# Modulation units dealt anew under the in-projection of layer 0, with the statistics, states and reload of layer 1 in new places

## The chip, the cores and the metric

The kernel runs on one core of a Trainium2 chip. The metric is the device time of one execution in microseconds (us). Engines are called as in the profile: PE is the matrix engine (TensorE), PEld its weight loads, DVE the vector engine, ACT the scalar engine, POOL is GpSimd, and SP issues most DMAs. Each engine works through its own queue in order; semaphores tie the queues together.

## The reference, cut to what matters

Two layers work on 512 latent rows and 256 context rows, both 2048 wide. Every layer is modulated: from the conditioning vectors come shift, scale and gate, `silu(c) @ ada_w[i] + ada_b[i]`, once for the latent rows and once for the context rows.

```python
for i in range(DEPTH):
    shift, scale, gate = jnp.split((sc @ ada_w[i] + ada_b[i])[:, None, :], 3, axis=-1)
    shift_c, scale_c, gate_c = jnp.split(scc @ ada_w[i] + ada_b[i], 3, axis=-1)
    h = rmsnorm(x, norm_w[i]) * (1.0 + scale) + shift
    hc = rmsnorm(xc, norm_w[i]) * (1.0 + scale_c) + shift_c
    ...
    x = x + gate * y
    if need_ctx:
        xc = xc + gate_c * yc
return rmsnorm(x, final_norm)
```

Layer 0 (`even_mix`) projects `h` and `hc` into a pool branch, its gate, low-rank queries and keys, and a gate of 1536 columns, then runs dense attention with 12 heads, and projects out. Layer 1 (`odd_mix`) projects into a bidirectional mLSTM with 4 heads (queries, keys, values, gates; the context rows give its initial states) and a window attention with 16 heads over 128-row windows plus the context keys, each with a Silu gate; then it projects out, for the latent rows alone.

## The kernel before, in words

Everything is computed transposed: features on the 128 partitions, rows along the free axis, in 16 chunks of 128 features. A float32 product is made of three matmuls with operands split into a high and a low half (`split`, lines 107 to 109: ACT writes the high half, DVE or POOL subtracts for the low half). Weights come in 512 KB pieces through `load_w` (line 111): three raw buffers, and four buffers each for high and low halves of half a piece.

**Modulation.** The columns of `ada_w` are cut into 24 units of 512 columns, 12 per layer. Units 0 to 7 (shift and scale of layer 0) are done on PE at the start. The others are done in one of two ways. `ada_pe_steps` (line 154) loads a unit in 16 pieces of 256 KB and multiplies them on PE, four pieces side by side in the array. `ada_vec_steps` (line 174) does it on DVE: per piece one `scalar_tensor_tensor` per conditioning vector adds the scaled piece to an accumulator (line 187), then a transpose and a reduction per accumulator (lines 192 and 193), and one tiny matmul folds the result (line 199). Units 20 to 23 (the gate of layer 1) need one vector alone, since layer 1 makes no context output: 17 steps with one operation each, where other units have 18 steps with two. A `Background` object (line 204) holds a row of such units; `bg.step(n)` at a place in the program text emits n steps there, `bg.finish()` the rest.

**In-projection of layer 0** (lines 480 to 603). `in_group(g, between, steps)` (line 505) does a group of 256 columns: four weight pieces, and for each 48 matmuls on 512 latent and 256 context rows, with `steps[0]` background steps before them and `steps[1]` behind. Order of groups: 2 and 3 (low-rank queries), 4 to 7 (pool branch and its gate, two and two, with the pool averages on DVE between), 8 to 13 (the attention gate). Before, the background of this stage held units 8 to 13, and groups 8 and 9 held units 18 and 19 on PE.

**Layer 0 to layer 1.** The out-projection of layer 0 adds into the residual and sums squares chunk by chunk on POOL, the last chunk on DVE (line 891). `stats1(v)` (line 926) turns the sums into one factor per row: tiny matmuls into `ps6b`, a root, and a broadcast by matmul. v is 0 for latent rows, 1 for context rows. `h_chunk` (line 278) then makes the modulated, normed, split input: HX for latent rows, HC for context rows. After that `x_group_t` (line 966) makes the mLSTM queries in two groups, from HX alone.

**mLSTM states.** `od_mv0`, the keys, then `mv_group` for value heads 1 to 3 and a last group with the window keys and values (lines 1199 to 1246). Between their weight pieces `next(state)` advances `ctx_state` (line 1214): scale the context values by their weights on DVE, split, six matmuls into `pc0`, split the result into `C0`; twice per head, for the two directions. Units 20 to 23 were the background of this stage.

**Window attention** (lines 1442 to 1701). A software pipeline over 4 head groups and 4 windows: scores of the next window (`Softmax.heads`), transposed probabilities and values of the present one (`w_values`), and between them `run(n)` takes n matmuls from `fillers()`: the query and gate projections of head groups 1 to 3 (`w_proj`), then the first out-projection groups (`out_steps`), which read Z, the split output of both branches. `z_load` (line 1558) reloads from DRAM the chunks of Z that are already made. `wq_split` (line 1458) rotates a finished query block (`do_rope`: shuffle, two products, a sum) and splits it.

The order of the instructions on each engine is settled when the program is built. A planner takes, by its own estimates of durations, the ready instruction that stands first in the program text; parts under `high_priority` go ahead, and where `manual_schedule` is set for PE (the window attention, the dense attention and the start), PE's order is the written one. Buffers of one tag are given out in turn. The planner does not see the chip: an instruction that is late there holds all that stands behind it in its queue.

Of the kernel before, what the change touches and what calls it, by code (L numbers as in the profile page):

```python
# [11 lines left out]
ALU = mybir.AluOpType  # L12
# [26 lines left out]
def tile_hybrid_dit(ctx: ExitStack, tc: tile.TileContext, ts: dict, out: bass.AP, dbg=None, upto=99):  # L39
# [94 lines left out]
    def ada_steps(u, pp, tp, nb=3, nt=2):  # L134

        pa = pp.tile([P, 512], F32, name=f"pa{u}", tag="pm")
        for q in range(4):
# [7 lines left out]
            if q == 3:  # L145
                tr = tp.tile([P, 16, 32], F32, name=f"ga{u}", tag="ga", bufs=1)
                V.transpose(tr.rearrange("p b r -> p (b r)"), pa)
                yield
                pb = pp.tile([32, 2, 16], F32, name=f"pb{u}", tag="pm")
                T.matmul(pb, fold, tr[:, :, 0:2].rearrange("p b v -> p v b"), start=True, stop=True)  # L150
                ada_place(u, pb, 2)
            yield

    def ada_pe_steps(u, pp, tp, nb):

        pa = pp.tile([P, 512], F32, name=f"pa{u}", tag="pm")
        for q in range(4):
            at = []
            for i in range(4):
                kc = 4 * q + i  # L160
                at.append(tp.tile([P, 512], F32, name=f"at{u}_{kc}", tag="ada", bufs=nb))
                DM.dma_start(at[i], ts["ada"][u, kc // 2][:, (kc % 2) * 512 : (kc % 2) * 512 + 512])
            for qd in range(4):
                T.matmul(pa[32 * qd : 32 * qd + 32, :], st[:, 4 * q + qd, :], at[qd], start=q == 0, stop=q == 3, skip_group_check=True)
            if q == 3:
                tr = ta("gat", 512).rearrange("p (b r) -> p b r", r=32)
# [162 lines left out]
    def do_rope(ps, r, tmp):  # L329
# [7 lines left out]
        G.tensor_tensor(t2, sw, rope[1], op=ALU.mult)  # L337
# [165 lines left out]
    bg = Background(range(8, 14), pp, ap_, 4, "ta", 6)  # L503
# [15 lines left out]
    for g in range(2):  # L519
        px, pc = in_group(2 + g, steps=(2, 2))  # L520
        raw += c_evac([(px[b], pc[:, b, :]) for b in range(2)], ssq)
# [50 lines left out]
    for pr in range(2):  # L572
        px, pc = in_group(4 + 2 * pr, steps=(1, 0))
# [9 lines left out]
        qx, qc = in_group(5 + 2 * pr, (lambda: mean(1), lambda: mix(0), lambda: None, lambda: mix(1)), (0, 0))  # L583
# [8 lines left out]
    for i in range(6):  # L592
        if i < 2:
            pe = ada_pe_steps(18 + i, pp, ap_, 4)
            px, pc = in_group(8 + i, (lambda: next(pe), lambda: next(pe), lambda: next(pe), lambda: (next(pe), next(pe))), (0, 0))
        else:
            px, pc = in_group(8 + i, steps=(2, 2))
# [344 lines left out]
    HX = [(hxp.tile([P, NX], F32R, name=f"hxh{j}"), hxp.tile([P, NX], F32R, name=f"hxl{j}")) for j in range(KC)]  # L942
# [33 lines left out]
    stats1(1)  # L976
    for j in range(KC):
        h_chunk(j, x1[j], ssq1, 12, 1, *((None, HC[j][i]) for i in range(2)), Ring(htp, 2), (1,))
    for i in range(2):
        for b, px in enumerate(x_group_t(G_MQ + i)):  # L980
# [214 lines left out]
    ea = ExitStack()  # L1195
    bg = Background(range(20, 24), pp, opool(ea, "ada1"), 4, "atr", 1)


    def mv_group(h, state):
        px, pc = new_px(2), new_pc()  # L1200
        pv = [px[b // 2][:, 256 * (b % 2) : 256 * (b % 2) + 256] for b in range(4)]
        for kq in range(4):
            w = load_w(odw[1 + h, kq])
            kcs = range(4 * kq, 4 * kq + 4)
            bg.step(2)
            kmode(pv, w, kcs, HX, kq == 0, kq == 3, 2)
            bg.step(3)
            kmode([pc[:, b, :] for b in range(2)], w, kcs, HC, kq == 0, kq == 3, 2)
            if kq % 2 == 0:
                next(state, None)  # L1210
# [28 lines left out]
    for kq in range(4):  # L1239
        w = load_w(odw[5, kq])  # L1240
        bg.step(2)
        tmode(px, [pc[:, b, :] for b in range(2)], w, range(4 * kq, 4 * kq + 4), HX, HC, kq == 0, kq == 3)
        if kq % 2 == 0:
            next(state, None)
    bg.finish()
    ea.close()
# [211 lines left out]
    def wq_split(src):  # L1458
        rr = ap2.tile([P, NX], F32, name="wrr", tag="wrr", bufs=1)
        do_rope(src, rr, rtmp(ap2))  # L1460
# [20 lines left out]
    def w_proj(i):  # L1481

        for g in (G_AQ + i, G_AZ + i):
# [5 lines left out]
            for kq in range(4):  # L1489
                w = load_w(odw[g, kq])  # L1490
                kcs = range(4 * kq, 4 * kq + 4)
                for b in range(2):
                    yield from steps(px, w, kcs, (b,), HX, kq == 0, kq == 3)
                    if kq == 3 and g < G_AZ:
                        qs[i] += wq_split(px[b])
                    elif kq == 3:
                        S.activation(zg[i][:, b, :], px[b], AF.Silu)
# [5 lines left out]
    class Softmax:  # L1503
# [7 lines left out]
        def heads(self, pair):  # L1511
# [12 lines left out]
            for a, s in zip(pair, ss_):  # L1524
                pr = wt("wpr_", 640)
                mx = tiny.tile([P, 1], F32, name="wm1", tag="wm1", bufs=4)
# [377 lines left out]
```

## Time and profile before

| | |
|---|---|
| three runs | 2303.32, 2305.13, 2306.37 us; median 2305.13 us |
| profiled execution | 2305.76 us, its span (first to last instruction) 2304.0 us |
| PE, PEld, DVE, ACT, POOL busy in the span | 2229.1, 1894.9, 1406.7, 916.3, 162.8 us |
| granted PE clock, mean | 0.993 |
| DMA | 309.14 MB, mean 134 GB/s |

A group's row reads: line, engine, operation, output <- inputs, shape, count, then busy time, mean duration in ns, and idle time of the engine before it. A wait's row reads: who waited <- for whom: us in total, times, longest. A timeline row reads: start, duration, engine, line, operation, count, and in brackets the idle time of the engine before it and what ended it. Matmuls are pipelined: one of 512 columns lasts 0.40 us in the records, but the next starts 0.23 us later.

### The profile page before, as it was taken

What the parts mean: (1) busy time and instruction counts of PE and PEld (TensorE: products, weight loads), DVE (VectorE), ACT (ScalarE), POOL (GpSimd) and SP (SyncE); (2) the same over time, 40 slices, a digit from 0 to 9 for tenths busy, and PEclk for the clock granted to TensorE, in tenths of its full rate; (3) what the DMA queues carried; (4) which work ended last, traced back from release to release, by engine and by line L of the source; (5) the groups of instructions that cost most, each with busy time, mean ns of one, the idle gap of its engine ahead of it and who ended that gap; (6) DMA issues with size and microseconds to landing.
All of it is one profiled execution on the core that took longest, in us unless ns stands there. A gap on an engine that the chain in (4) does not pass through costs nothing. (4 is left out here: it accounts for less than half of the span.)

```text
span 2304.0 us, 34221 instructions
## 1 busy us (share of the span) xinstructions
PE 2229.1 (97%) x13000; PEld 1894.9 (82%) x13000; DVE 1406.7 (61%) x2841; ACT 916.3 (40%) x1864; POOL 162.8 (7%) x203
## 2 busy tenths in 40 slices
PE   5999999999999999999999999999999999999998
PEld 3678888788899999888888799988888878777887
DVE  5579523296666666788558524763455587778434
ACT  4232222112444444542226322223556667656432
POOL 0000100000000000011113100000000000003110
PEclk9999999999999999999999999999999999999999
DMA  9855323565211112276444321753232312113433
GB/s 386 322 202 179 121 85 115 185 227 186 100 49 54 51 56 69 101 252 224 160 158 154 93 100 65 247 185 120 88 101 94 103 61 68 65 55 122 135 113 116
DMA packets 118005, 309.14 MB, mean 134 GB/s; under 512 B 13612, under 2 KB 21292, under 8 KB 117840
## 3 DMA queue, kind: packets, MB, share of 16 engines
q1 hardware_dynamic: 110960, 279.64, 36.2%
q0 software_dynamic: 6880, 27.32, 3.2%
q8 instruction: 102, 1.67, 0.3%
q14 instruction: 63, 0.52, 0.1%
HBM read 277.28 MB, written 29.62 MB: 133 GB/s over the span
## 5 line engine op out<-in xcount | busy, mean ns | idle before, releaser
L108 ACT CAST wh<-wraw 128x512 fp32r<-128x512 f32 (+2 forms) x540 | 316.1, 590 | 852.5 <-PE pc L311 372.1
L109 DVE TENSOR_TENSOR wl<-wraw,wh 128x512 fp32r<-128x512 f32 (+2 forms) x540 | 358.5, 669 | 467.7 <-ACT wh L108 464.4
L187 DVE SCALAR_TENSOR_TENSOR acc<-at,st,acc 128x512 f32<-128x512 f32 x360 | 251.9, 749 | 25.8 <-DMA at<-in_ada_dram 24.2
L322 PE MATMUL px<-wh,hxh 128*128 128x512 f32 (+2 forms) x512 | 174.9, 342 | 0.8 <-ACT sz L1310 0.8
L322 PE MATMUL px<-wl,hxh 128*128 128x512 f32 (+2 forms) x512 | 174.0, 340 | 0.0
L322 PE MATMUL px<-wh,hxl 128*128 128x512 f32 (+2 forms) x512 | 173.9, 340 | 0.0
L309 PE MATMUL px<-h0h,wh 128*128 128x512 f32 x384 | 152.9, 398 | 0.0
L309 PE MATMUL px<-h0h,wl 128*128 128x512 f32 x384 | 151.7, 395 | 0.3 <-DVE wl L109 0.3
L309 PE MATMUL px<-h0l,wh 128*128 128x512 f32 x384 | 151.6, 395 | 0.0
L311 PE MATMUL pc<-h0h,wl 128*128 128x256 f32 x400 | 112.7, 282 | 0.0
L311 PE MATMUL pc<-h0h,wh 128*128 128x256 f32 x400 | 112.5, 281 | 0.0
L311 PE MATMUL pc<-h0l,wh 128*128 128x256 f32 x400 | 112.4, 281 | 0.0
L322 PEld LDWEIGHTS px<-wh,hxh 128*128 128x128 f32 x512 | 96.7, 189 | 13.6 <-ACT sz L1310 1.9
L322 PEld LDWEIGHTS px<-wl,hxh 128*128 128x128 f32 x512 | 96.7, 189 | 11.2
L322 PEld LDWEIGHTS px<-wh,hxl 128*128 128x128 f32 x512 | 96.6, 189 | 11.2
L309 PEld LDWEIGHTS px<-h0h,wh 128*128 128x128 f32 x384 | 72.1, 188 | 22.9 <-ACT wh L108 4.2
L309 PE MATMUL px<-hxh,wh 128*128 128x512 f32 x224 | 89.7, 400 | 0.0
L309 PE MATMUL px<-zxl,wh 128*128 128x512 f32 x224 | 89.3, 399 | 0.0
L309 PE MATMUL px<-hxl,wh 128*128 128x512 f32 x224 | 89.2, 398 | 0.0
L309 PE MATMUL px<-hxh,wl 128*128 128x512 f32 x224 | 89.1, 398 | 0.0
L309 PE MATMUL px<-zxh,wl 128*128 128x512 f32 x224 | 88.7, 396 | 0.0
L309 PE MATMUL px<-zxh,wh 128*128 128x512 f32 x224 | 88.2, 394 | 0.0
(887 smaller groups left out, 6010.1 us busy)
## 6 DMA issues: line engine op xcount, KB each, us to landing
at<-in_ada_dram SPq DMA_DIRECT2D x256, 256.0 KB, 3.4
at<-in_ada_dram SPq DMA_DIRECT2D x64, 512.0 KB, 7.9
wraw<-in_od_in_dram SPq DMA_DIRECT2D x64, 512.0 KB, 3.5
wraw<-in_ev_in_dram SPq DMA_DIRECT2D x56, 512.0 KB, 4.2
wraw<-in_ev_out_dram SPq DMA_DIRECT2D x44, 512.0 KB, 3.9
wraw<-in_od_oz_dram SPq DMA_DIRECT2D x32, 512.0 KB, 3.5
wraw<-in_od_out_dram SPq DMA_DIRECT2D x32, 512.0 KB, 3.5
xt<-in_xT_dram SPq DMA_DIRECT2D x16, 384.0 KB, 7.3
```

Of the source, the lines that this page charges most:

```text
L108: S.copy(h, src)
L109: low.tensor_tensor(l, src, h, op=ALU.subtract)
L187: V.scalar_tensor_tensor(a, at, st[:, kc, v : v + 1], a, op0=ALU.mult, op1=ALU.add)
L309: T.matmul(px[b], w_, Hx[kc][r_], start=s0, stop=s1)
L311: T.matmul(pc[b], w_, Hc[kc][r_], start=s0 and b == 0, stop=s1, skip_group_check=True)
L322: T.matmul(p_, h_, w_, start=s0, stop=s1, skip_group_check=True)
```

## The change

- Units 18 and 19 are no longer done on PE: `ada_pe_steps` is removed. Units 20 to 23 leave layer 1. All of them join the background of the in-projection of layer 0, twelve units in the order 8, 9, 20 to 23, 10 to 13, 18, 19. The steps per weight piece there are 2 and 1 in groups 2 and 3, 2 and 2 in the pool groups, 3 and 2 in groups 8 to 13.
- The context statistics and the HC chunks stand behind the first mLSTM query group in the text.
- `ctx_state` is advanced behind the second and fourth weight piece of a group instead of the first and third.
- HX tiles get tags, and Z takes over their buffers tile by tile. Chunks 0 to 7 of Z are reloaded during the last gate projection, 8 to 13 before their use as before; the reload splits on ACT and DVE instead of DVE and POOL.
- The rotation of the window queries runs on DVE alone; the product with the sine was POOL's.
- The window gate copies its first block out as it is, and does both Silus when the second is there.
- The two maxima of a score pair are taken one after the other, and one operation forms the bias of both.
- 16 fillers instead of 8 stand ahead of the second score pair of the first window, 12 instead of 20 behind it.

```diff
-    def ada_pe_steps(u, pp, tp, nb):
...
-                T.matmul(pa[32 * qd : 32 * qd + 32, :], st[:, 4 * q + qd, :], at[qd], start=q == 0, stop=q == 3, skip_group_check=True)
...
-    def do_rope(ps, r, tmp):
+    def do_rope(ps, r, tmp, eng=G):
...
-        G.tensor_tensor(t2, sw, rope[1], op=ALU.mult)
+        eng.tensor_tensor(t2, sw, rope[1], op=ALU.mult)
...
-    bg = Background(range(8, 14), pp, ap_, 4, "ta", 6)
+    bg = Background((8, 9, 20, 21, 22, 23, 10, 11, 12, 13, 18, 19), pp, ap_, 4, "ta", 6)
...
-        px, pc = in_group(2 + g, steps=(2, 2))
+        px, pc = in_group(2 + g, steps=(2, 1))
...
-        px, pc = in_group(4 + 2 * pr, steps=(1, 0))
+        px, pc = in_group(4 + 2 * pr, steps=(2, 2))
...
-        qx, qc = in_group(5 + 2 * pr, (lambda: mean(1), lambda: mix(0), lambda: None, lambda: mix(1)), (0, 0))
+        qx, qc = in_group(5 + 2 * pr, (lambda: mean(1), lambda: mix(0), lambda: None, lambda: mix(1)), (2, 2))
...
-        if i < 2:
-            pe = ada_pe_steps(18 + i, pp, ap_, 4)
-            px, pc = in_group(8 + i, (lambda: next(pe), lambda: next(pe), lambda: next(pe), lambda: (next(pe), next(pe))), (0, 0))
-        else:
-            px, pc = in_group(8 + i, steps=(2, 2))
+        px, pc = in_group(8 + i, steps=(3, 2))
...
-    HX = [(hxp.tile([P, NX], F32R, name=f"hxh{j}"), hxp.tile([P, NX], F32R, name=f"hxl{j}")) for j in range(KC)]
+    HX = [tuple(hxp.tile([P, NX], F32R, name=f"hx{n}{j}", tag=f"hx{n}{j}") for n in "hl") for j in range(KC)]
...
-    stats1(1)
-    for j in range(KC):
-        h_chunk(j, x1[j], ssq1, 12, 1, *((None, HC[j][i]) for i in range(2)), Ring(htp, 2), (1,))
     for i in range(2):
-        for b, px in enumerate(x_group_t(G_MQ + i)):
+        pxs = x_group_t(G_MQ + i)
+        if i == 0:
+            stats1(1)
+            for j in range(KC):
+                h_chunk(j, x1[j], ssq1, 12, 1, *((None, HC[j][n]) for n in range(2)), Ring(htp, 2), (1,))
+        for b, px in enumerate(pxs):
...
-    bg = Background(range(20, 24), pp, opool(ea, "ada1"), 4, "atr", 1)
...
-            bg.step(2)
             kmode(pv, w, kcs, HX, kq == 0, kq == 3, 2)
-            bg.step(3)
             kmode([pc[:, b, :] for b in range(2)], w, kcs, HC, kq == 0, kq == 3, 2)
-            if kq % 2 == 0:
+            if kq % 2:
                 next(state, None)
...
-        do_rope(src, rr, rtmp(ap2))
+        do_rope(src, rr, rtmp(ap2), V)
...
+                    elif kq == 3 and b == 0:
+                        S.copy(zg[i][:, 0, :], px[0])
                     elif kq == 3:
-                        S.activation(zg[i][:, b, :], px[b], AF.Silu)
+                        S.activation(zg[i][:, 1, :], px[1], AF.Silu)
+                        S.activation(zg[i][:, 0, :], zg[i][:, 0, :], AF.Silu)
+                    if g == G_AZ + 3 and 3 <= 2 * kq + b < 7:
+                        z_load(2 * (2 * kq + b - 3))
...
-            for a, s in zip(pair, ss_):
-                pr = wt("wpr_", 640)
-                mx = tiny.tile([P, 1], F32, name="wm1", tag="wm1", bufs=4)
-                V.tensor_tensor_reduce(pr[:, :nk], s[:, 512 - nl : 768], mk[:, :nk], 1.0, -3e38, ALU.add, ALU.max, mx)
-                V.scalar_tensor_tensor(self.nmx[:, a : a + 1], mx, -A_SCALE, nsink[:, 4 * i + a : 4 * i + a + 1], op0=ALU.mult, op1=ALU.min)
+            mx = tiny.tile([P, 2], F32, name="wm1", tag="wm1", bufs=2)
+            prs = [wt("wpr_", 640) for _ in pair]
+            for n, s in enumerate(ss_):
+                V.tensor_tensor_reduce(prs[n][:, :nk], s[:, 512 - nl : 768], mk[:, :nk], 1.0, -3e38, ALU.add, ALU.max, mx[:, n : n + 1])
+            a = pair[0]
+            V.scalar_tensor_tensor(self.nmx[:, a : a + 2], mx, -A_SCALE, nsink[:, 4 * i + a : 4 * i + a + 2], op0=ALU.mult, op1=ALU.min)
+            for a, pr in zip(pair, prs):
                 S.activation(pr[:, :nk], pr[:, :nk], AF.Exp, bias=self.nmx[:, a : a + 1], scale=A_SCALE, accum_out=self.ssm[:, a : a + 1])
...
-                for j in range(4 * kq, 4 * kq + n, 2):
+                for j in range(max(8, 4 * kq), 4 * kq + n, 2):
                     z_load(j)
...
-            h, l = Z[j + i]
-            V.tensor_copy(h, raw[:, 512 * i : 512 * i + 512])
-            G.tensor_tensor(l, raw[:, 512 * i : 512 * i + 512], h, op=ALU.subtract)
+            z_place(j + i)
+            split(raw[:, 512 * i : 512 * i + 512], *Z[j + i])
+
+    def z_place(j):
+
+        Z[j] = tuple(hxp.tile([P, NX], F32R, name=f"z1{n}{j}", tag=f"hx{n}{j}") for n in "hl")
...
-    PRE, PRE2, PRE3, RATE, RATE_END = 16, 8, 20, 9.5, 13
+    PRE, PRE2, PRE3, RATE, RATE_END = 16, 16, 12, 9.5, 13
```

More of the change, by code (lines that the diff above doesn't have):

```diff
@@ L146, in ada_steps @@
                 tr = tp.tile([P, 16, 32], F32, name=f"ga{u}", tag="ga", bufs=1)
[L147 to L152, printed above, removed]
-    def ada_pe_steps(u, pp, tp, nb):
[L156 to L166, printed above, removed]
                 V.transpose(tr.rearrange("p b r -> p (b r)"), pa)
@@ L1192, in tile_hybrid_dit @@
     eg.close()
-    ea = ExitStack()
-    bg = Background(range(20, 24), pp, opool(ea, "ada1"), 4, "atr", 1)
     def mv_group(h, state):
@@ L1240, in tile_hybrid_dit @@
         w = load_w(odw[5, kq])
-        bg.step(2)
         tmode(px, [pc[:, b, :] for b in range(2)], w, range(4 * kq, 4 * kq + 4), HX, HC, kq == 0, kq == 3)
-        if kq % 2 == 0:
+        if kq % 2:
             next(state, None)
-    bg.finish()
-    ea.close()
     for b in range(2):
@@ L1561, in z_load @@
             DM.dma_start(raw[:, 512 * i : 512 * i + 512], z1d[j + i])
-            h, l = Z[j + i]
-            V.tensor_copy(h, raw[:, 512 * i : 512 * i + 512])
-            G.tensor_tensor(l, raw[:, 512 * i : 512 * i + 512], h, op=ALU.subtract)
+            z_place(j + i)
+            split(raw[:, 512 * i : 512 * i + 512], *Z[j + i])
+    def z_place(j):
+        Z[j] = tuple(hxp.tile([P, NX], F32R, name=f"z1{n}{j}", tag=f"hx{n}{j}") for n in "hl")
     def fillers():
-        nonlocal Z, ezf
         for i in range(1, 4):
             yield from w_proj(i)
-        ehx.close()
-        ezf = ExitStack()
-        zp = opool(ezf, "zp1", side="right")
-        Z = [(zp.tile([P, NX], F32R, name=f"z1h{j}"), zp.tile([P, NX], F32R, name=f"z1l{j}")) for j in range(KC)]
+        for j in (14, 15):
+            z_place(j)
         pxs.append(new_px2())
@@ L1580, in fillers @@
             yield from out_steps(g, pxs[g])
-    PRE, PRE2, PRE3, RATE, RATE_END = 16, 8, 20, 9.5, 13
-    Z = ezf = None
+    PRE, PRE2, PRE3, RATE, RATE_END = 16, 16, 12, 9.5, 13
+    Z = [None] * KC
     pxs, ends = [], []
@@ L1771, in tile_hybrid_dit @@
     eF.close()
-    ezf.close()
+    ehx.close()
     esP.close()
```

## The prediction

> **What bounds the kernel now.** I read the page's busy times first, then the windows by stage, then TensorE's waits.
>
> ```profile
> span 2304.0 us, 34221 instructions
> PE 2229.1 (97%) x13000; PEld 1894.9 (82%) x13000; DVE 1406.7 (61%) x2841; ACT 916.3 (40%) x1864; POOL 162.8 (7%) x203
> ```
> ```profile
> 165.00:590.00 425.00, 423.79 (x2438) 361.20 (x2438) 246.97 (x400) 97.18 (x173) 18.49 (x31) 1.00 0.47 154
> 1255.00:1282.00 27.00, 22.58 (x96) 18.19 (x96) 20.24 (x38) 11.98 (x23) 8.18 (x6) 0.87 0.35 112
> 1436.00:1546.00 110.00, 105.23 (x845) 102.66 (x844) 83.41 (x155) 26.06 (x48) 1.74 (x5) 0.98 0.69 225
> 1838.00:2118.00 280.00, 265.59 (x1352) 214.12 (x1351) 215.32 (x496) 181.51 (x347) 35.54 (x29) 0.99 0.23 76
> ```
>
> Columns: stretch, length, busy time of PE, weight load, DVE, ACT, POOL, then granted clock, DMA share, GB/s. TensorE is full nearly everywhere, so only two things can shorten the kernel: fewer TensorE instructions, or the holes it still has. The in-projection (165 to 590) has 1.2 us of holes. The change touches three stretches that have some: 4.4 us around the layer-1 statistics, 4.8 us in the state stage, 14.4 us in the window attention. Who is late there:
>
> ```profile
> PE wpo L1651 <- DVE wpl L109: 5.1, 6, 1.3
> PE ps6b L267 <- DVE ssq L891: 4.6, 2, 4.4
> PE pc L1228 <- ACT wvh L108: 3.9, 1, 3.9
> PE px L1478 <- POOL z1l L1564: 1.4, 3, 0.5
> PE px L1478 <- ACT wzg L1497: 0.9, 1, 0.9
> ```
>
> The sum is made against the profiled execution: 2305.76 us, of which 2304.0 are the span. The median of the runs is 2305.13, 0.6 less.
>
> **Part A, units 18 and 19 leave TensorE; units 20 to 23 come in.** Removed is the line-164 group below, 8.5 us in a stretch where TensorE has no hole; its two folds on line 170 are replaced by two folds on line 199 (4 records each, 0.2 us a record), no difference. I take **-8**, because some 0.5 us of the 8.5 overlaps the neighbours.
>
> ```profile
> L164 PE MATMUL pa<-at,st 128*32 128x512 f32 x64 | 8.5, 605 | 0.0
> L187 DVE SCALAR_TENSOR_TENSOR acc<-at,st,acc 128x512 f32<-128x512 f32 x114 | 77.6, 745 | 4.3 <-DMA at<-in_ada_dram 4.1
> ```
> ```profile
> 455.00:589.00 134.00, 134.00 (x775) 116.81 (x773) 106.62 (x177) 26.75 (x49) 3.79 (x8) 1.00 0.60 199
> ```
> ```profile
> 509.94 3.39 DVE L187 SCALAR_TENSOR_TENSOR acc<-at,st,acc 128x512 f32<-128x512 f32 x5
> ...
> 532.49 1.42 DVE L187 SCALAR_TENSOR_TENSOR acc<-at,st,acc 128x512 f32<-128x512 f32 x2 [0.20 <-DMA at<-in_ada_dram]
> ```
>
> The work lands on DVE. An accumulation costs 77.6/114 = 0.68 us there; a step is two of them (1.36) for units 8 to 19 and one for units 20 to 23. The background grows from 108 steps to 212 (8 units of 18, 4 of 17). In the four pool groups 64 steps stand where 8 stood, 12 of them double and 52 single: 12 x 1.36 + 52 x 0.68 - 8 x 1.36 = 41 us more. Groups 8 and 9 get 16 single and 24 double steps, 44 us, where none stood. For these the in-projection has room: DVE is busy 247 of its 425 us, and least in these six groups. The tight place is the last four groups (455 to 589): 80 steps for 64, 16 x 1.36 = 22 more, so 106.6 + 22 = **128 of 134 us**. I hold that this still hides, for two reasons. DVE already ran a unit's 16 steps without a break from 509 to 534, with six weight splits between, in 25 us, and TensorE lost nothing; a group has 33.5 us, and the unit's two transposes and reductions (2.6) and two more splits (1.3) fit too. And the low halves of the weights have four buffers, each half feeding TensorE for some 4 us, so a split may be late by about three halves. On SP the 64 loads of units 20 to 23 are issued between the weight loads of this stage; the 32 of units 18 and 19 only change line. Bounds: 0 to +5, the late end of a few pool mixes and of the last unit's transposes, behind which the next stage's splits queue; I take **+1**. If the cover is gone altogether it is the slower rival below.
>
> **Part B, statistics behind the first query group.**
>
> ```profile
> 1269.19 0.40 PE L309 MATMUL px<-hxl,wh 128*128 128x512 f32 x1
> 1269.43 0.40 PE L309 MATMUL px<-hxh,wl 128*128 128x512 f32 x1
> 1274.24 0.98 PE L267 MATMUL ps6b<-od,ssq 128*128 128x1 f32 x4 [4.42 <-DVE ssq L891]
> ...
> 1277.37 0.63 PE L309 MATMUL px<-hxh,wl 128*128 128x512 f32 x1
> 1277.80 0.63 PE L309 MATMUL px<-hxh,wh 128*128 128x512 f32 x1
> ```
> ```profile
> 1279.12 0.42 DVE L261 COPY ssq<-prs 128x256 f32<-128x256 f32 x1 [2.49 <-PE prs L260]
> ...
> 1298.16 0.48 DVE L292 SCALAR_TENSOR_TENSOR hcl<-ht,av,hch 128x256 fp32r<-128x256 f32 x1
> ```
>
> TensorE was inside the query group when the statistics took their place in its queue, and stood 4.4 us for the last squares. Behind the hole seven matmuls start 0.43 us apart instead of 0.24, the last at 1277.80: 1.4 us, and the statistics' own four about 0.4. With 96 matmuls in the group, 36 of them (8.4 us) still to come at 1269.4, the squares of 1274 are there in time. What is late next: the context chunks, 19 us of DVE from 1279 to 1298. They would start about 1281 and end about 1301; the second query group ends near 1302, and the first context matmul comes 3 us later. So nothing new is exposed, and the term is 4.4 + 1.4 + 0.4 = **-6** (bounds: -6.5, and 0 if the planner puts the statistics where they were).
>
> **Part C, state stage without background.**
>
> ```profile
> 1490.67 0.59 ACT L1029 COPY vcx<-pc 128x512 f32<-128x512 f32 x1 [0.83 <-PE pc L322]
> ```
> ```profile
> 1498.09 1.54 DVE L187 SCALAR_TENSOR_TENSOR acc<-at,st,acc 128x512 f32<-128x512 f32 x2 [3.83 <-DMA at<-in_ada_dram]
> ...
> 1501.59 0.61 DVE L1219 TENSOR_SCALAR wv<-vcx,wcol 128x258 f32<-128x258 f32 x2
> ```
> ```profile
> 1502.91 0.38 PE L1228 MATMUL pc<-wvh,mkch 128*128 128x258 f32 x1 [3.94 <-ACT wvh L108]
> 1504.12 0.58 PE L1228 MATMUL pc<-wvl,mkch 128*128 128x258 f32 x1 [0.83 <-DVE wvl L109]
> ```
>
> The values lay ready at 1491.3, but the scaling waited ten microseconds in DVE's queue behind an accumulation that waited for its modulation weights. Without these, scaling and split are done near 1493.5, and the matmul moreover comes a quarter of a group later. The holes of the whole stage go (4.8), and with them the half-speed matmuls behind: a granted clock of 0.98 over 110 us is 2.2 us of lost clock, of which I count 1.7, the rest falling into the hole itself: **-6.5** (bounds -7, -4). The second state of the last group now follows the last projection directly; that is 0.7 us of matmul moved.
>
> **Part D, window attention.** Four edits.
>
> ```profile
> 2030.00:2052.00 22.00, 19.00 (x86) 15.09 (x85) 16.80 (x37) 10.30 (x20) 2.55 (x2) 0.84 0.10 31
> 2080.00:2118.00 38.00, 32.50 (x158) 24.17 (x157) 35.06 (x67) 24.21 (x47) 19.75 (x14) 1.00 0.43 139
> ```
> ```profile
> 2082.24 6.46 DVE L1563 CAST z1h<-wraw 128x512 fp32r<-128x512 f32 x6
> ```
>
> The reload: six copies hold DVE for 6.4 us while POOL subtracts, the low halves of the probabilities queue behind, and 2080 to 2118 has 5.5 us of holes. Eight of fourteen chunks now come during the last projection, whose first half has released their buffers, and the split is 0.6 us on ACT and 0.68 on DVE with POOL silent. The other six still come at need: **-5** (bounds -5.5, -1).
>
> ```profile
> 1929.83 0.21 ACT L1537 ACTIVATE wes<-wes 128x4 f32<-128x4 f32 x1
> 1930.06 1.28 ACT L1497 ACT_TABLE_LOAD   x1
> 1931.35 0.60 ACT L1497 ACTIVATE wzg<-px 128x512 f32<-128x512 f32 x1
> ```
>
> The gate: a plain copy frees the first accumulator, and the pair's two Silus stand together, so the wait of 0.9 us goes: **-1**. [...]
>
> The rotation moves from POOL to DVE:
>
> ```profile
> 1842.08 1.79 DVE L335 TENSOR_TENSOR rt<-aq,rope 128x512 f32<-128x512 f32 x1
> ```
> ```profile
> 1841.71 1.61 POOL L337 TENSOR_TENSOR rt<-rsw,rope 128x512 f32<-128x512 f32 x1 [1.49 <-DVE kro L338]
> ```
>
> DVE pays about 0.6 us more, eight times, and no longer runs 1.1 us long beside POOL. [...] At the worst place, 2030 to 2052 (3.0 us of holes and a clock of 0.84), the added work and the removed wait are about equal: **0** (bounds -6, +5). Joining the two maxima saves a 0.15 us operation per pair and delays the first exponential by the second maximum, 0.7 us; scaled probabilities are ready 1.2 us before use in the tight windows:
>
> ```profile
> 1882.04 0.83 ACT L1543 ACTIVATE wpr__19001<-wpr__19001,wr 128x640 f32<-128x640 f32 x1
> ```
> ```profile
> 1884.03 0.27 PE L1640 MATMUL wpt<-con,wpr__18945 128*128 128x128 f32 x1
> ```
>
> So that hides with 0.5 us to spare. Moving eight fillers ahead of the second pair changes no count: 0.
>
> **Sum.** -8 + 1 - 6 - 6.5 - 5 - 1 = -25.5 on 2305.8 gives 2280.3; less 0.6 to stand beside the median, **2279.5 us**.
>
> **The rivals.** *The window attention does not gain* (D at 0): the reload's 5 us return as new waits, since DVE, 215 of 280 us busy there, keeps its backlog and now rotates too. For it: the worst hole lies in a rotation, not a reload. Against: POOL's copies vanish. 2285.5.
>
> *The window attention gains twice*: with the rotation no longer split over two engines, the holes of 2030 to 2052 and some at 1838 to 1866 go as well, 6 to 9 us with the slow clock behind them. 2272.
>
> *The statistics stay where they were* (the change does not do what it says): only the written order changes, and the planner may again find them ready. Against: 36 matmuls with precedence then stand ahead of them. 2285.5.
>
> *Slower: the in-projection becomes DVE-bound.* The place is the last four groups, with 6 us left of 134. Waits for modulation weights come on top:
>
> ```profile
>   DMA at<-in_ada_dram: 4.1, 5
> ```
> ```profile
>   DMA at<-in_ada_dram: 17.2, 14
> ```
>
> The first is today's 455 to 589, the second the state stage, 1436 to 1546. At today's rate 2 us are left. At the state stage's rate, 17.2 per 110, the 134 us would hold 21 us, 15 too many, and the two groups before as much again by half; that alone eats 22 of the gain (no change, 2303). It decides for slower from about 32 us of waits in the 134; at twice the state stage's rate, 42 us, the loss is 36 x 1.5 = 54 and the time 2333. Against: the DMA share was 0.69 there and 0.60 here, growing with 16 loads in 74 to about 0.7, but a step here is 1.36 us against 0.68, so four buffers cover twice as long.
>
> **How the numbers follow.** Forecast 44%, no gain in D 18%, double gain in D 18%, statistics unmoved 8%, in-projection bound 12% (5 near no change, 7 slower). The forecast's own range is 2275 to 2285; to hold 8 in 10 I reach to both D cases: 2266 to 2290. About 0.2%, 4.6 us, is what a measurement of this kernel can tell from no change: faster 0.88, same 0.05, slower 0.07.
>
> **What would show it.** A: no line 164, the windows of 455 to 589 with PE full and DVE near 96%. B: no wait of ps6b above 1 us and the clock at 1.00 there. C: no wait of line 1228. D: wpo's wait for wpl under 3 us and no POOL in 2080 to 2118. I am wrong if TensorE waits for wl in the in-projection, or if the holes of the window attention only move.

## The result

| | before | changed |
|---|---|---|
| runs of the comparison | 2303.32 to 2309.93 us (6), median 2305.81 | 2276.95 to 2285.29 us (6), median 2282.86 |
| ratio | | 0.9894, 95% interval 0.9877 to 0.9910 |
| profiled execution | 2305.76 us, span 2304.0 | 2278.7 us, span 2276.9 |
| a second comparison, later | median 2306.22 (11 runs) | median 2282.99 (6 runs), ratio 0.9896 (0.9879 to 0.9912) |

The change saves 23 us at the median, 27.1 in the two profiled spans; forecast were 25.5. Where some of the 4 us between median and profile come from is told in the last section.

For reading stage by stage I cut each span at the start of a matmul: the last gkr, the first pj, the first px<-zx, the first with HX, the first with HC, the first bc, the first pvt, the last s<-z1. All stage times below are differences of such starts. "Again" is a second trace of the unaltered changed kernel, "best" the last version of the experiments.

| stretch, us | before | changed | again | best |
|---|---|---|---|---|
| start-up | 156.9 | 159.7 | 158.1 | 156.0 |
| A: in-projection of layer 0 | 433.2 | 421.8 | 427.8 | 427.8 |
| attention of layer 0 | 410.6 | 409.9 | 410.1 | 410.4 |
| out-projection of layer 0 | 255.1 | 256.8 | 257.0 | 257.0 |
| B: first HX to first HC | 55.4 | 48.7 | 48.7 | 48.7 |
| C: first HC to first bc (states) | 264.5 | 255.3 | 256.5 | 255.1 |
| mLSTM | 281.3 | 282.5 | 284.0 | 282.5 |
| D: window attention | 319.5 | 313.8 | 314.8 | 306.0 |
| end | 127.6 | 128.5 | 128.1 | 128.6 |

### The profile page after: what moved, and what is told of

Same layout as the page of the kernel before. It is cut to its first block, busy times and chain, and to the rows that moved or that the text cites. A ratio compares the mean times of both kernels' runs of the same rounds, so it can differ in the third digit from the quotient of the medians.

```text
span 2276.9 us, 34143 instructions
## 1 busy us (share of the span) xinstructions
PE 2212.0 (97%) x12936; PEld 1887.7 (83%) x12936; DVE 1442.6 (63%) x2885; ACT 924.1 (41%) x1883; POOL 132.4 (6%) x181
## 4 chain that ended last, share of the span: by engine, by line
PE 91%; DVE 5%; ACT 2%; issue 1%; DMA 1%; POOL 0%; SPq 0%; DVEq 0%; ACTq 0%; POOLq 0%
PE px L289 31%; PE px L302 11%; PE pc L291 10%; PE pj L622 5%; PE px L1448 5%; PE s L685 4%; PE pc L302 3%; PE om L728 3%; PE px L361 2%; PE pj L642 2%; PE s L1448 2%; PE po L1361 2%; PE tp L710 2%; PE pa L143 1%; PE pc L362 1%
## 5 line engine op out<-in xcount | busy, mean ns | idle before, releaser
L167 DVE SCALAR_TENSOR_TENSOR acc<-at,st,acc 128x512 f32<-128x512 f32 x420 | 293.4, 748 | 26.9 <-DMA at<-in_ada_dram 25.3
L289 PEld LDWEIGHTS px<-h0h,wl 128*128 128x128 f32 x384 | 72.1, 188 | 16.3
```

Of the source, the lines that this page charges most:

```text
L167: V.scalar_tensor_tensor(a, at, st[:, kc, v : v + 1], a, op0=ALU.mult, op1=ALU.add)
L289: T.matmul(px[b], w_, Hx[kc][r_], start=s0, stop=s1)
```

## The profile after

The page's busy times, then the windows that answer the four shown of before (same columns, each stretch moved with its stage):

```profile
PE 2212.0 (97%) x12936; PEld 1887.7 (83%) x12936; DVE 1442.6 (63%) x2885; ACT 924.1 (41%) x1883; POOL 132.4 (6%) x181
```
```profile
168.00:581.50 413.50, 412.57 (x2383) 359.56 (x2381) 341.39 (x557) 99.21 (x175) 18.56 (x31) 1.00 0.61 199
1247.50:1274.50 27.00, 27.00 (x125) 21.99 (x124) 20.66 (x37) 13.48 (x26) 9.26 (x8) 1.00 0.46 155
1422.00:1532.00 110.00, 110.00 (x884) 107.32 (x884) 35.13 (x76) 26.92 (x49) 1.74 (x5) 1.00 0.22 77
1816.00:2096.00 280.00, 269.14 (x1384) 219.16 (x1383) 212.22 (x489) 192.99 (x374) 4.73 (x7) 0.99 0.23 78
```

PE lost 64 instructions, the line-164 group. DVE has 341 of 413 us to do in the in-projection and TensorE has 0.9 us of holes in it. The holes at the statistics and in the state stage are gone, with the clock back at 1.00. The window attention keeps 10.9 of its 14.4 us of holes. TensorE's waits there, first of the kernel before (beside the three that the prediction shows), then of the changed one:

```profile
PE s L1522 <- DVE wm L1527: 2.1, 2, 1.9
PE s L1522 <- ACT az L1436: 2.0, 1, 2.0
PE wpo L1650 <- DVE wzt L1658: 1.7, 2, 1.0
```
```profile
PE s L1497 <- DVE wm L1502: 5.4, 2, 3.2
PE px L1448 <- ACT wzg L1469: 2.9, 2, 1.5
PE wpo L1628 <- DVE wpl L109: 0.5, 2, 0.2
```

The reload's wait (wpl) went from 5.1 to 0.5, the waits for az and wzt left; but the wait of the scores for the maxima grew from 2.1 to 5.4, and that for the gate from 0.9 to 2.9. The longest hole, with DVE's queue of those microseconds:

```profile
2018.12 0.28 PE L1498 MATMUL s<-KLw,wq 128*128 128x256 f32 x1
2021.58 0.55 PE L1497 MATMUL s<-KHw,wq 128*128 128x256 f32 x1 [3.18 <-DVE wm L1502]
```
```profile
2016.33 0.69 DVE L1502 CUSTOM_DVE_ANT_0 wpr__20716<-s,msk 128x512 f32<-128x512 f32 x1
...
2016.96 0.74 DVE L314 STREAM_SHUFFLE rsw<-px 128x512 f32<-128x512 f32 x1
2017.59 0.68 DVE L315 TENSOR_TENSOR rt<-px,rope 128x512 f32<-128x512 f32 x1
2018.29 0.69 DVE L1436 TENSOR_TENSOR wq<-wrr,wq 64x512 fp32r<-64x512 f32 x1
2018.99 0.69 DVE L109 TENSOR_TENSOR wpl<-wpt,wph 128x512 fp32r<-128x512 f32 x1
2019.69 0.69 DVE L1436 TENSOR_TENSOR wq<-wrr,wq 64x512 fp32r<-64x512 f32 x1
2020.39 0.42 DVE L1636 TENSOR_TENSOR wzt<-wzt,wzg 128x256 f32<-128x256 f32 x1
2020.74 0.68 DVE L1502 CUSTOM_DVE_ANT_0 wpr__20717<-s,msk 128x512 f32<-128x512 f32 x1
```

The first maximum is taken at 2016.3, the second 4.4 us later: between them stand, beside wpl and wzt, four operations of a rotation and its split, whose result is not read before 2037, some 16 us later. The second score's accumulator stays occupied that long.

## The experiments

### A: the block's price, and the cover

Units 18 and 19 back on PE:

```diff
+        if i < 2:
+            pe = ada_pe_steps(18 + i, pp, ap_, 4)
+            px, pc = in_group(8 + i, (lambda: next(pe), ...), (0, 0))
```

> The changed kernel with units 18 and 19 back on PE under groups 8 and 9; all else as changed. In the traces so far groups 8 and 9 take 38.39 and 38.90 us with the two units on PE and 33.65 each without, so a block of eight 128x32 matmuls costs 10.0/8 = 1.25 us and not the 1.07 of its busy time. Theory (the whole block price, DVE costs nothing): the in-projection (from the last gkr matmul to the first pj matmul) goes from 421.8 to about 432, all of it in groups 8 and 9. Rival (the prediction's sizes, 8 saved and 1 lost to DVE): 429, with groups 10 to 13 shorter than 33.65 each now that DVE has 48 us less to do.

Measured: groups 8 and 9 take 38.39 and 39.08 us, 10.2 more than the 67.3 of the changed kernel; the whole stage takes 436.8. So eight blocks cost close to 10 us, although the group's row reads as in the kernel before:

```profile
L164 PE MATMUL pa<-at,st 128*32 128x512 f32 x64 | 8.7, 605 | 0.0
```

From its first start to the first start behind it a block lasts 1.0 us (385.29 to 386.29 in the kernel before), and the matmuls on both sides of it start 0.1 us late: 1.2 a block, 9.6 in all. The other 5 us of this trace are not the blocks: 2.0 come with a wait of the next stage for the last unit (2.9 us; the late end that the prediction bounded by 0 to +5), 2.8 with a slower pace in groups 4 to 7 and 10, of which more below. Groups 11 and 12 took the same 33.65 us with less for DVE to do: the rival's half, that DVE costs something there, falls.

One more accumulation, whose result nobody reads, in the steps of units 20 to 23, and in a second kernel in those of the other eight:

```diff
                     V.scalar_tensor_tensor(a, at, st[:, kc, v : v + 1], a, op0=ALU.mult, op1=ALU.add)
+                if u >= 20:
+                    V.scalar_tensor_tensor(at, at, st[:, kc, 0:1], at, op0=ALU.mult, op1=ALU.add)
```

> The changed kernel with one more accumulation (a scaled piece, whose result nobody reads) in 15 steps of each of units 20 to 23: 60 x 0.68 = 41 us more DVE in the in-projection, 349 + 41 = 390 of 421.8. Theory (DVE works through the background ahead of its place in the text, so the cover is the 73 us of the whole stage): the stage stays within 1 us of 421.8. Rival (the cover is local: groups 4 to 7 have some 9 us of DVE left each and get 10 more, group 8 had 1 us left): 3 to 8 us longer, with waits of PE for wl in groups 4 to 8.

> The changed kernel with one more accumulation (result not read) in 15 steps of each of the eight two-vector units: 120 x 0.68 = 82 us, 349 + 82 = 431 of 421.8, so DVE must become the bound here. Theory (the whole stage covers): about 10 us longer plus a few for stretches with no background, 432 to 437. Rival (the cover is local: groups 2 and 3 have 2 us of DVE left and get 20 more, groups 8 to 13 have 27 left and get 61): 18 + 34 = about 52 us longer, 474. In both PE waits for wl, as the slower case of the prediction had it.

Measured with the smaller load, the window of the stage and TensorE's only wait in it:

```profile
164.50:582.50 418.00, 416.95 (x2380) 360.67 (x2378) 378.57 (x616) 98.96 (x174) 18.48 (x31) 1.00 0.61 196
```
```profile
PE ppx L551 <- DVE wpooll L109: 0.4, 1, 0.4
```

DVE is busy 379 of 418 us, and TensorE waits for no weight of the in-projection; the 0.4 us are for the small weight of the pool branch. The stage's 426.8 us miss the theory's 421.8 by 5, but lie within the spread of traces without the load: groups 8 to 12 ran at the slower pace, 34.25 to 34.28 us each. With the larger load:

```profile
165.00:608.50 443.50, 420.42 (x2378) 362.57 (x2376) 414.87 (x670) 99.74 (x176) 19.75 (x33) 0.98 0.57 188
```
```profile
PE px L291 <- DVE wl L109: 14.7, 9, 3.6
PE pj L644 <- DVE av L131: 8.4, 1, 8.4
```

The stage takes 452.6 us and the next one 6.9 more; the kernel 2312.85 us in one run, 5.9 us above the kernel before in the one run beside it (2306.99). Neither theory had its size (432 to 437, 474). Nothing is lost until 485 us: groups 2 to 10 keep their time (of the 30 us from 445 on DVE is busy 29.9, TensorE all). Then groups 11, 12 and 13 take 38.9, 41.4 and 52.1. So the cover is not the sum of the stage, and not each group either: a backlog is carried on as long as buffers are in front of TensorE, and comes due at the end. The slower rival is thus a real mechanism with the symptom that it was given (wl), and the point from which it decides lies between 41 and 82 us of further DVE work.

### B: the statistics put back

```diff
+    stats1(1)
+    for j in range(KC):
+        h_chunk(j, x1[j], ssq1, 12, 1, ...)
     for i in range(2):
         pxs = x_group_t(G_MQ + i)
-        if i == 0:
-            stats1(1)
-            ...
```

> The changed kernel with the context statistics and HC chunks back ahead of the first query group in the text. Theory (the place in the text sets the hole): the wait of ps6b for the last squares is back at 4 us or more with half-speed matmuls behind it, and the stretch from the first HX matmul to the first HC matmul goes from 48.7 to about 55 us. Rival (the 6.7 us came from the squares of this stage being earlier for another reason): the stretch stays below 51.

Measured 55.55 us (48.73 as changed), and the hole:

```profile
1270.14 0.98 PE L247 MATMUL ps6b<-od,ssq 128*128 128x1 f32 x4 [4.08 <-DVE ssq L868]
```

The same stretch of the changed kernel shows the same four matmuls without one:

```profile
1270.64 0.50 PE L247 MATMUL ps6b<-od,ssq 128*128 128x1 f32 x4
```

The place in the text is worth 6.8 us. The rival falls.

### C and the joined maxima

```diff
-            if kq % 2:
+            if kq % 2 == 0:
                 next(state, None)
...
-            mx = tiny.tile([P, 2], F32, name="wm1", tag="wm1", bufs=2)
+                mx = tiny.tile([P, 1], F32, name="wm1", tag="wm1", bufs=4)
...
```

> The changed kernel with two parts far apart put back, each read in its own stretch: the states advance behind the first and third weight piece again (the units stay out of this stage), and every score block has its own maximum and its own bias operation. State stage (first HC matmul to first bc matmul, 255.3 us as changed, 264.5 before). Theory, as predicted: the gain is the modulation work that left DVE's queue, and the quarter of a group is worth nothing: 255 to 256 and no wait of the state's matmul above 1 us. Rival: the later place is what lets scaling and split finish in time: a wait of 1 us or more comes back at each head, 258 or more. Window attention (first pvt to last s<-z1 matmul; 311.9 to 314.5 in the five traces in which this part is as changed): theory, joined maxima are worth nothing, 312 to 315; rival, the second maximum ahead of the bias holds DVE back in the tight windows and the waits of s for wm (5.4 us) shrink, 309.

State stage: 257.9 us, and no wait of the state's matmul; TensorE's only wait in the stage is

```profile
PE bc L1306 <- ACT selh L1258: 0.9, 1, 0.9
```

(0.4 as changed). Of the 2.6 us more, 0.6 are five matmuls that now stand on this side of the mark; the next stage is 0.9 shorter. Taken over both, the early place costs at most 1.7 us, and not by the wait that the rival named: 0.5 of them are the longer wait of bc, which the unaltered kernel shows with 0.4 us in one trace and 1.7 in another. Window attention: 312.4 us, inside the spread of 311.9 to 314.5, with s waiting 5.6 us for wm as before the edit. The joined maxima are worth nothing, as predicted.

### C's units and the reload, both put back

```diff
+            bg.step(2)
             kmode(pv, w, kcs, HX, kq == 0, kq == 3, 2)
+            bg.step(3)
...
-                    if g == G_AZ + 3 and 3 <= 2 * kq + b < 7:
-                        z_load(2 * (2 * kq + b - 3))
...
-            split(raw[:, 512 * i : 512 * i + 512], *Z[j + i])
+            V.tensor_copy(h, raw[:, 512 * i : 512 * i + 512])
+            G.tensor_tensor(l, raw[:, 512 * i : 512 * i + 512], h, op=ALU.subtract)
```

> The changed kernel with two other parts put back, each read in its own stretch: units 20 to 23 are the background of the state stage again (the states keep their new place), and all fourteen Z chunks are reloaded at need and split on DVE and POOL. State stage: theory, scaling queues on DVE behind accumulations that wait for their weights, so the wait of the state's matmul is back at 1 to 4 us with half-speed matmuls behind it: 259 to 264 against 255.3; rival, with the states a quarter of a group later the background does not reach them: 255 to 256.5. In-projection: 69 us less DVE there, the same time within the spread of its traces (421.8 to 427.8), since it is covered. Window attention: theory, as predicted, waits of wpo for wpl come back from 0.5 to 4 us or more and the stretch goes from 313.8 to about 318; rival, the holes only move, 312 to 315.

State stage: 262.2 us, 7.0 of the 9.2 are back, but the late one is not the state's matmul. The waits of the stage, and DVE at the first of them:

```profile
PE px L302 <- DVE wl L109: 2.9, 3, 1.0
PE px L289 <- DVE wl L109: 1.8, 1, 1.8
```
```profile
1483.31 2.33 DVE L167 SCALAR_TENSOR_TENSOR acc<-at,st,acc 128x512 f32<-128x512 f32 x3 [1.00 <-DMA at<-in_ada_dram]
1485.55 0.69 DVE L109 TENSOR_TENSOR wl<-wraw,wh 128x512 fp32r<-128x512 f32 x1
```

The accumulations wait for their modulation weights, and whatever stands behind them is late: the scaled values with the states in the old place, a weight split with them in the new one. So most of the gain of C is the work that left DVE's queue. The in-projection, without those units, took 425.8 us, inside its spread. Window attention: 314.2 us, and

```profile
PE wpo L1636 <- DVE wpl L109: 4.3, 4, 1.6
PE px L1456 <- ACT wzg L1477: 1.5, 1, 1.5
```

The wait for wpl is back at 4.3, but one of the two waits for the gate (1.3 us, at 2066 as changed) is gone: 12.9 us of holes instead of 10.9. The half-speed matmuls behind the longest hole stayed away (last section), which hides most of these 2 us: the stretch is 0.4 us longer, inside the spread. So the rival has the number, and by its holes the reload is worth some 2 us here, not 5.

### The rotation

```diff
-        do_rope(src, rr, rtmp(ap2), V)
+        do_rope(src, rr, rtmp(ap2))
```

> The changed kernel with the sine product of the rotation on POOL again. Window attention. Theory (formed on the trace after: at 1951 and 2018 TensorE stands 2.3 and 3.3 us because the score maxima queue on DVE behind the operations of a rotation): with a product less in DVE's queue these two waits shrink from 5.4 to about 3 us in all, and the stretch from 313.8 to 310. Rival (the prediction's, POOL beside DVE makes DVE's operations 1.1 us longer and that was the cost): the waits are as long or longer, 314 to 317.

Measured 316.3 us, 2.5 more, of which 1.5 are holes (12.3 us instead of 10.9). The theory had its wait right, and forgot the others that come in its place; the rival has the number, but not by the waits for the maxima:

```profile
PE s L1497 <- DVE wm L1502: 2.4, 2, 1.9
PE s L1497 <- ACT az L1406: 1.8, 1, 1.8
PE wpo L1628 <- DVE wpl L109: 1.7, 3, 1.1
PE wpo L1627 <- DVE wzt L1635: 1.7, 2, 1.0
```

What the prediction had said of DVE beside POOL is half right. Durations (min/median/max, ns) of the cosine product in this kernel:

```profile
L315 DVE TENSOR_TENSOR rt<-px,rope x6: 666/674/678, 1871.7 to 2026.5; 128x512 f32<-128x512 f32 x6
L315 DVE TENSOR_TENSOR rt<-aq,rope x2: 1786/1788/1789, 1823.9 to 1834.0; 128x512 f32<-128x512 f32 x2
```

Only the two products that read aq from SBUF run long beside POOL; the six that read the accumulator px do not. That the source decides it is not proved: in the trace of before, with the same durations, the two long ones start 0.4 us behind POOL's product, the six short ones 0.25 us ahead of it, and a ninth that reads ak from SBUF, 0.35 us ahead, took 0.68 us too. What speaks for the source is POOL's own time there, 1.27 to 1.30 us beside px, 1.49 beside ak and 1.61 beside aq. The prediction let the 1.1 us saved stand against 0.6 us more, eight times; they had been paid at two of the eight.

### The gate

```diff
-                    elif kq == 3 and b == 0:
-                        S.copy(zg[i][:, 0, :], px[0])
                     elif kq == 3:
-                        S.activation(zg[i][:, 1, :], px[1], AF.Silu)
-                        S.activation(zg[i][:, 0, :], zg[i][:, 0, :], AF.Silu)
+                        S.activation(zg[i][:, b, :], px[b], AF.Silu)
```

> The changed kernel with each gate block's Silu taken straight from its accumulator again. Window attention. Theory (from the trace after: the wait of px for the second Silu is 2.9 us in two places, 0.9 before): the gate edit cost about 2 us, so the wait falls to 1 and the stretch from 313.8 to about 312. Rival (the prediction's -1): the wait is there anyway, as the Silu stands behind four exponentials, and one more table load per head group comes on top: 314 to 316.

Measured 310.9 us, 2.9 less and below every trace with the edit (311.9 us or more), and

```profile
PE px L1448 <- ACT wzg L1467: 1.4, 2, 0.9
```

The edit cost some 2 us: 1.5 of the 2.9 are this wait, 0.7 lie in shorter waits of pvt and wpl, which need not be the edit's. ACT in the changed kernel, where TensorE waits from 1907.9 to 1909.4:

```profile
1900.20 1.28 ACT L1470 ACT_TABLE_LOAD   x1
1901.49 0.63 ACT L1470 ACTIVATE wzg<-wzg 128x512 f32<-128x512 f32 x1
...
1907.24 0.19 ACT L1514 ACTIVATE wes<-wes 128x4 f32<-128x4 f32 x1
1907.45 1.28 ACT L1469 ACT_TABLE_LOAD   x1
1908.74 0.60 ACT L1469 ACTIVATE wzg<-px 128x512 f32<-128x512 f32 x1
```

The second block's accumulator is freed by its Silu, the Silu stands behind four exponentials, and the table load is between them. The copy of the first block is not in this chain. Nor do the two Silus stand together, though the edit was meant to do both when the second block is there: the first block's (line 1470) was ready behind its copy, and the planner put it there, 7 us ahead of the second's (line 1469), with a table load of its own. The whole trace has 37 table loads before, as changed and with the edit undone, so the rival's further load per head group falls, and the edit added a copy and saved nothing.

### Versions that go further

First the changed kernel once more, then two versions: the maxima and the bias under high priority, both gate blocks copied out under high priority with one Silu over the pair; the second version also has more fillers ahead (20, 16, 18).

```diff
+            with tc.high_priority():
                 for n, s in enumerate(ss_):
                     V.tensor_tensor_reduce(prs[n][:, :nk], ...)
...
+                        with tc.high_priority():
+                            S.copy(zg[i][:, b, :], px[b])
+                        if b == 1:
+                            S.activation(zg[i], zg[i], AF.Silu)
```

> The changed kernel itself, unaltered, for its spread and as the neighbour of the two versions below. In nine traces with this change the in-projection was 421.8 us once and 425.8 to 427.8 in the six others that share its program, with TensorE full and the clock at 1.00 in all: a pair of matmuls (512 and 256 columns) is repeated after 346.7 ns in the one and after 352 to 353.4 ns in the others. Theory (two paces of the same program, chosen at a break in the stream): this trace shows one of the two, 421.8 or about 427.8, and the runs spread over 6 us or more. Rival (the first trace of the changed kernel was special in its program): 421.8 again and a narrow spread.

Measured: the in-projection takes 427.8 us, the second of the two paces, and the runs go from 2277.43 to 2286.91 us. The theory holds; the table above has the other stages.

> The changed kernel with two edits in the window attention: the score maxima and the bias go ahead of all other DVE work that is ready (as the split of the transposed probabilities does), and both gate blocks are copied out of their accumulators at once, with one Silu over both behind it. Theory: the two waits of s for wm (5.4 us, half-speed matmuls behind them 2.3 us) and the waits of px for wzg (2.9 us) go; what is late next is the rest of the rotation, whose queries are needed some 20 us later, so nothing: the stretch from the first pvt to the last s<-z1 matmul goes from 313.8 to about 305, the time to about 2275 beside the changed kernel's own runs here. Rival (holes only move, as the reload's did): the split of the probabilities or the sums wzt are late instead, 311 or more.

> As the version before, and 20 instead of 16 fillers ahead of the first scores, 18 instead of 12 behind the second score pair of the first window. Theory: the holes ahead of the first pvt (0.6 to 1.0 us) and ahead of the first transposed probabilities (1.2 us) are covered by matmuls that would otherwise run at the end: 1.5 to 2 us less than the version before. Rival: the fillers' accumulators and rotations come earlier against the scores and make a new hole: no gain.

The first version's median is 2279.47 us (5 runs), the stretch 310.4; the second's 2281.88 (6 runs), 316.2. The waits aimed at are gone, the rival took most of it: in the first version

```profile
PE wpo L1628 <- DVE wzt L1636: 6.0, 5, 3.2
```

and 8.1 in the second, where more fillers ahead also made a new hole of 3.4 us at 1869 instead of covering 1.5 to 2. One Silu over the pair brings the table loads of the trace from 37 to 33. The sums that empty the output accumulator now stood behind the rotation. Last, they too go ahead of it:

```diff
+            with tc.high_priority():
                 S.copy(lo, po[64:128, :])
                 for e in range(2):
                     V.tensor_tensor(zt[64 * e : 64 * e + 64, :, qq], v3(po), v3(lo), op=ALU.add)
```

> The version with early maxima and copied gate blocks, and the copy and the sums that free the output accumulator (wlo, wzt) ahead of other DVE and ACT work as well. In that version the waits of s for wm and of px for wzg were gone, but wpo waited 6.0 us for the sums wzt, since they stood behind the rotation in DVE's queue. Theory (with all that TensorE waits for ahead of the rotation, the rotation itself has 20 us of room): the waits for wzt fall from 6.0 to under 2 us and the window stretch from 310.4 to about 306, the time to some 2275. Rival (DVE's queue is in the order of the planner's estimates, the chip's DVE is behind them at each rotation, and some other operation is late instead): waits of 4 us or more in all in this stretch, 309 to 312, and the time as that version's, 2279.

Measured: median 2274.53 us (2272.22 to 2275.47, 4 runs), 0.9863 of before (0.9843 to 0.9882), 8.3 us under the changed kernel's median (measured at another time; the two intervals just overlap); the stretch 306.0, and

```profile
1819.00:2099.00 280.00, 274.81 (x1422) 222.81 (x1422) 214.74 (x497) 194.65 (x378) 4.75 (x7) 1.00 0.24 79
```
```profile
PE wpo L1628 <- DVE wzt L1637: 2.2, 5, 0.6
```

5.2 us of holes instead of 10.9, the longest 1.0 us, the clock at 1.00; DVE does as much as before (215 of 280). The theory holds, with 2.2 us left where it had under 2: what cost was not DVE's load but the order of its queue.

## Why the prediction was right, and where not

**The total** is right: 23 us at the median for 25.5. Of its terms B and C are right in their mechanism, A in what it removes, and D is right only as a sum.

**A, forecast -7.** Measured -11.4 in one trace and -5.4 in the other (again). The step "removed is the group's 8.5 us" was too small: a block costs its neighbours 1.2 us, 9.6 in all. The +1 for DVE was not paid, since TensorE's one wait in the stage is 0.9 us at its end, as before. "128 of 134 in the last four groups" was wrong as well:

```profile
448.00:580.00 132.00, 132.00 (x763) 115.21 (x762) 111.92 (x189) 27.48 (x48) 3.24 (x6) 1.00 0.62 201
402.00:437.00 35.00, 35.00 (x204) 30.37 (x204) 34.14 (x60) 7.34 (x13) 1.08 (x2) 1.00 0.76 245
```

It was 112 of 132: a part of the 80 steps ran earlier, in groups 8 and 9, where DVE is full (34.1 of 35) and TensorE still loses nothing. A step's place in the text is its rank, not its time. The rest is the pace of TensorE, which the prediction did not know, and the one trace of before is at the faster pace from group 10 on, like the first changed one:

```profile
480.00:510.00 30.00, 30.00 (x174) 26.34 (x174) 28.74 (x50) 6.71 (x13) 1.08 (x2) 1.00 0.68 229
```

So the -11.4 compares nearly like with like, and the -5.4 a faster pace with a slower one.

**B, forecast -6:** -6.7, and 6.8 when undone. All its steps stood: wait 0.4, clock 1.00, nothing late behind it.

**C, forecast -6.5:** -9.2 (-8.0 again). The holes and the slow clock were seen; left out were the eight tiny fold matmuls of the four units (0.7 us with the gaps that they make) and five matmuls at the mark (0.6), which the mLSTM stage pays, and the three late matmuls cost 5.4 from start to start, where the waits read 4.8. The moved place of the states, which the prediction counted as part of the reason, is worth at most 1.7 of it.

**D, forecast -6:** -5.7 (-4.6 again), by other terms. *Reload, -5:* its waits went as predicted, but undone it costs 0.4, or 2 by the holes. The step that failed is the sum itself: it added terms that share one queue. *Gate, -1:* a loss of some 2; the step "a plain copy frees the first accumulator, so the wait goes" looked at the block that was not late, and "the pair's two Silus stand together" did not happen. In the rows above the second table load takes 1.28 us, begins 0.02 us after the operation before it, and the Silu starts 0.01 us behind it. *Rotation, 0:* -2.5, inside its bounds. *Joined maxima:* 0.

Undone one by one the parts come to no gain at all (0.4 + 2.5 - 2.9), but six traces with this part unaltered go from 311.9 to 314.8 us, so each of these is near the spread. By holes the stage gained 3.5 of the 5.7 (14.4 to 10.9), and the parts 1.3 (2.0 + 1.5 - 2.2). The rest lies in their combination, in the fillers ahead of the second pair, which were not tried alone, or in the pace; that stays open. The rival "the reload's 5 us return as new waits" described the mechanism better than the forecast did, though the stage gained. The prediction's own sign of being wrong, holes that only move, came true in part: the waits for wpl, az and wzt shrank by 8.3 us, those for the maxima and the gate grew by 5.3.

**Slips in the working.** 2280.3 less 0.6 is 2279.7, not 2279.5. The slower rival, at the prediction's own estimate of 1.5 us lost per us of waits over 6, would decide from about 26 us of waits (30.2 / 1.5 + 6), not 32. The scaled tile of the rows for the joined maxima, wpr__19001, is read at 1884.36, so it was ready 1.5 us before use, not 1.2. None of them changes the forecast.

**What balanced.** In the first trace A and C gave 7 more than forecast, and start-up, out-projection, mLSTM and end 6.6 us less (+2.9, +1.7, +1.2, +0.8), so that the first trace comes within 2 us of the forecast is partly luck. Start-up varies by itself, 156.0 to 159.7 in the traces. The out-projection is 255.7 to 257.1 in all thirteen traces with the change, against 255.1 in the one trace of before. The 1.7 us are holes, 4.2 us instead of 2.6, half of the difference in a wait for the residual x at the end of the stage (1.6 instead of 0.8); why it is later stays open. Half of the mLSTM's 1.2 are the five matmuls.

## What to carry to other kernels

Two edits that feed the same in-order queue are not to be added: take the holes of a stage together, and ask of each operation in the queue who waits for it and for how long it may be late; the ones that free an accumulator go first (TensorE's waits for wzt fell from 6.0 to 2.2 us), a rotation that is needed some 15 us later goes last. Text that is written to run together need not: look in the trace where the planner put it. What a block of small matmuls costs is read from start to start of its neighbours, not from its busy time (here 1.2 us a block, 1.07 by its row in the kernel before). And before a stage's gain is believed to a per cent, a second trace of the same kernel (421.8 and 427.8 us here).

## What the runs showed of the hardware

**Two paces of a full TensorE.** The in-projection alternates matmuls of 512 and 256 columns. In the first trace of the changed kernel a pair is repeated every 346.7 ns, in the second after 346 and 361 ns by turns, 353.3 in the mean; with PE full and the clock at 1.00 in both, the same program, 30 us hold 175 or 171 instructions:

```profile
480.00:510.00 30.00, 30.00 (x175) 26.18 (x174) 28.16 (x47) 5.90 (x11) 1.08 (x2) 1.00 0.68 223
```
```profile
480.00:510.00 30.00, 30.00 (x171) 25.88 (x170) 27.12 (x46) 6.71 (x12) 1.08 (x2) 1.00 0.63 204
```

A group takes 33.65 or 34.27 us, and the stage 421.8 or 427.8. The pace stays for hundreds of us and changes where other matmuls come in between: in the first changed trace 30 us hold 172 instructions from 200 us on, ahead of the statistics at 241, and 174 or 175 wherever they are read from 265 to 580; in the kernel before 172 or 173 from 200 to 360, 174 or 175 from 460 on, behind the blocks of units 18 and 19. In the changed kernel with units 18 and 19 back on PE, groups 4 to 7 had the slower pace and 11 and 12, behind the last of the blocks, the faster one. Of the nine traces whose in-projection is this program, two have the shorter, seven the longer. That is 6 of the 8.2 us between the two traces of the changed kernel. It is likely, but not shown, since the other runs left no trace, that it is also why its runs spread (2276.95 to 2286.91) and why its first profiled run (2278.7) lies below the median. What chooses the pace stays open.

**The half clock is not a function of the hole's length.** At the rotation of the last head group TensorE stood 3.18 us in the changed kernel and 3.17 in the one with the old reload. The 6 us behind the hole, in this order:

```profile
2021.50:2027.50 6.00, 5.92 (x17) 4.68 (x18) 4.40 (x10) 2.64 (x6) 0.00 (x0) 0.52 0.00 0
```
```profile
2030.40:2036.40 6.00, 5.89 (x30) 4.89 (x31) 5.87 (x14) 3.92 (x9) 0.00 (x0) 1.00 0.00 0
```

The granted clock was 0.52 in one, 1.00 in the other. Some 2 us hang on it, as an estimate from the stretches: the trace with the old reload has 2.0 us more of holes and is 0.4 us longer, and the trace with units 18 and 19 back on PE, which runs the same window attention, takes 311.9 us where the first changed trace takes 313.8 (mean clock of the whole spans 0.996 and 0.994). What decides which clock follows is not shown, and a hole of 3.2 us is to be priced with both bounds, with the slow clock behind it and without.
